# One hybrid attention and feed-forward layer: the first dilated head's preparation, the constant fills and the raw output weights are moved

## The chip, the cores and the metric

The kernel runs on one core of one Trainium2 chip. The metric is the device time of one execution in microseconds; the median of several runs is compared. The core has five engines with queues of their own: TensorE (PE, with its weight loads as PEld), VectorE (DVE), ScalarE (ACT), GpSimd (POOL) and SyncE (SP), which here issues nearly all DMA transfers.

## The reference

One encoder layer over 1024 positions of width 1024, in float32:

```
proj = rms_norm(x, norm1_g) @ w_in            -> qA(512) kA(128) vA(128) qB kB vB (512 each)
out_a = dense softmax attention: 8 q heads, 2 kv heads, QK-norm, 2-D axial rotary
out_b = 8 heads, mixture of three dilated windows (128,1) (512,4) (2048,16), ALiBi, QK-norm
x = x + concat(rms_norm(out_a), rms_norm(out_b)) @ w_out
u = conv3(rms_norm(x, norm2_g) @ w_up) + conv_b
out = x + (gelu(u[:2816]) * u[2816:]) @ w_down
```

## The kernel before, in words

All data lie in two hand-placed arenas in SBUF (`bigf` for float32, `bigr` for float32r) and one in PSUM (`ps`, eight banks); the constants O_..., F_..., R_... at the top of the file are places in them, and several tenants share a place one after another. A float32 product is made of three float32r products: each operand is split into a high part (a ScalarE copy) and a low part (a subtraction on VectorE or GpSimd).

The stages, with their time in the profile:

- *In-projection*, to about 212 us: four column chunks, seven block products each (`in_product`), with the weights prepared two products ahead (`w_prep`: a subtraction such as L382, the copy L388, the subtraction L389), results taken out of PSUM by `in_out` (ACT L420 to L428, DVE L417), and the norm and rotary of finished q and k (`done`: L490 norm, L285 turn on GpSimd, L500 and L503). Beside the last chunk the dense keys are split and transposed (`k_split` L324, `k_ready` with the transposes L177 and the ScalarE copies L332 and L333), four constants of -1 are written under the keys (`fill_k`, L348), and the first dense group is prepared.
- *Dense heads*, about 212 to 431 us: 16 groups of 13.4 us (128 queries by 4 heads). `a_prep(g + 1)` hands out the preparation of the next group in seven pieces: `nat` (L576, L577), `first` (transposes), four row maxima `mx` (products L597, maxima L598), `last` (L601, transposes, L605). `a_main(g, ...)` goes over eight key tiles: scores (L624, L625), exponential (L627), one or more pieces of the preparation according to the tuple `plan`, and the products with V of two tiles before (L619); `o_norm` (L639, L640) writes the group's output to `qab`. Group 15 prepares the first dilated head in place of a further group: 16 pieces, `b_split(0)` and the fifteen of `b_prep(0)`.
- *Dilated heads*, about 431 to 600 us: eight heads of some 20 us, eight steps each. `b_split` splits k and q of a head, `b_prep` transposes q (`trq`, copy L700) and k (`trk`, ScalarE copies L691 and L692, VectorE casts L693 and L694), takes eight row maxima (`mx`, products L707 to L712, maxima L718) and transposes the corrected low parts of q (`trl`: L726, transposes, copy L731). `b_s` makes the scores of a step: bias L747, then L759 and L761 (first four steps) or L769 and L770, the exponential L773, and for the first four steps a split (copy L775, subtraction L776). L761 and L770 read what `trl` wrote. `b_pv`, two steps behind, multiplies with V (L790, L795; out of PSUM by L798 and L802 into F_OS). The next head's `b_prep` is handed out beside the steps.
- *Output projection* to about 700 us, then up-projection, convolution, gate and down-projection. The raw rows of w_out (eight blocks, `wo_load`, L812) are loaded into places that are free for a while (`F_WOR`) and split from there into `R_WO` (`wo_split`, ScalarE L818, VectorE L819); the table `wo_early` says at which head and step.

Constants that the dilated heads need (ones and zeros around V, zeros beside the low parts of q, -1 under the keys) are the nine `fills`, of which one is handed out behind each of the first nine dense groups. `fill` multiplies any finite data by zero and adds the constant (L214, 128 rows; L926 and L348, 64 rows).

What sets the order: each engine runs a fixed list. The lists are made ahead of time by the framework's planner, which takes the program text as priority and may put an instruction earlier than its place in the text when its data and its place are free in its own reckoning. Semaphores then hold an instruction until what it depends on is done; an engine does not pass a waiting instruction.

Of the kernel before, what the change touches and what calls it, by code (L numbers as in the profile page):

```python
# [32 lines left out]
O_IDF = 0  # L33
# [62 lines left out]
F_G2 = O_F + 3584  # L96
F_HN = O_F + 4608
F_JK3 = O_F + 7840
F_WOR = [O_F + o for o in (2560, 2560, 2560, 3584, 5632, 6656, 2560, 5632)]


R_T2 = R_W
# [21 lines left out]
def tile_encoder_layer(ctx, tc, x, w_in, gains, outg, norm1_g, norm2_g, w_out, w_up, conv_w, conv_b,  # L124
# [20 lines left out]
    def f(off, n):  # L145
        return bigf[:, off:off + n]

    def r(off, n):
        return bigr[:, off:off + n]
# [11 lines left out]
    def rp(off, *dims):  # L161
        return raw_ap(bigr[:, off:off + 1], dims)
# [46 lines left out]
    def qab(tt):  # L209
        return O_QAB + 1024 * tt  # L210

    def fill(dst, n, m, c):

        vec.tensor_scalar(dst, f(O_IDF, m)[:, None, :].to_broadcast([128, n, m]), 0.0, c, op0=OP.mult, op1=OP.add)  # L214

# [127 lines left out]

    def fill_k():
        for i in range(4):
            vec.tensor_scalar(r(R_KHA + 512 * i, 512)[64:128], f(F_ROPE, 512)[64:128], 0.0, -1.0,  # L348
                              op0=OP.mult, op1=OP.add)


    def w_buf(c, half):
# [227 lines left out]
    def a_prep(g):  # L580
        b, kv = divmod(g, 2)
        q2 = R_Q2A + 512 * (g % 2)
        ql = R_QLA + 512 * (g % 2)

        def nat():
            q_nat(qab(b) + 256 * kv, 64, vec, 4, 512 * kv)

        def first():
            t = next_tr()
            for i in range(4):  # L590
                tr_r(t, i, r(R_QD + 128 * (4 * kv + i), 128))
            act(r(q2, 512), bank(t), AF.Copy)

        def mx(i):
            for hf in range(2):
                b = hf
                mm(bank(b), r(q2 + 128 * i, 128), r(R_K2A + 1024 * kv + 512 * hf, 512), start=True, stop=True)  # L597
                vec.tensor_reduce(f(SM_MC + 8 * hf + i, 1), bank(b), axis=AX.X, op=OP.max)  # L598

        def last():  # L600
            vec.tensor_tensor(rp(R_QLN + 512 * kv + 64, [128, 4]), f(SM_MC, 4), f(SM_MC + 8, 4), op=OP.max)  # L601
            t = next_tr()
            for i in range(4):
                tr_r(t, i, r(R_QLN + 128 * (4 * kv + i), 128))
            act(r(ql, 512), bank(t), AF.Copy)  # L605

        return [nat, first] + [lambda i=i: mx(i) for i in range(4)] + [last]
# [65 lines left out]
    def b_split(h):  # L673
        k3 = fp(F_KN[h % 2], [64, 8], [1, 64])
        act(rp(R_KN, [128, 8], [1, 64]), k3, AF.Copy)
        gp.tensor_tensor(rp(R_KN + 64, [128, 8], [1, 64]), k3, rfp(R_KN, [128, 8], [1, 64]), op=OP.subtract)
        q_nat(O_QAB + 512 + 64 * h, 1024, gp, 8, 0, R_QLB[h % 2])
        if h < 6:
            load_k(h + 2)
# [237 lines left out]
        eng.tensor_tensor(r(o + 512, 512), t_raw(n, i), rf(o, 512), op=OP.subtract)  # L917


    fills = []  # L920
    for c, v in ((64, 1.0), (192, 0.0)):
        for i in range(2):
            fills.append(lambda o=R_VB + 1024 * i + c, v=v: fill(rp(o, [256, 4], [1, 64]), 4, 64, v))
    fills.append(lambda: fill(rp(R_QLB[1] + 64, [128, 8], [1, 64]), 8, 64, 0.0))
    for i in range(4):
        fills.append(lambda o=R_SET[0] + 2048 + 512 * i: vec.tensor_scalar(  # L926
            r(o, 512)[64:128], f(O_QAB, 512)[64:128], 0.0, -1.0, op0=OP.mult, op1=OP.add))

    def take(prep, n):
        for _ in range(n):  # L930
# [2 lines left out]
                if p:  # L933
                    p()

    prep = [lambda: fill(rp(R_QLN + 64, [128, 8], [1, 64]), 8, 64, 0.0)] + a_prep(0)
    for i in range(4):
        kv_proj(i)
        x_rest(i)
# [94 lines left out]
    load_tabs(1)  # L1034

    tail = []
    for g in range(16):
        prep = a_prep(g + 1) if g < 15 else [lambda: b_split(0)] + b_prep(0)
        tail = a_main(g, prep, tail, late, (3, 2, 2, 2, 2, 2, 2, 1) if g == 15 else (1, 1, 1, 1, 1, 1, 1, 0),
                      (0, 1, 1, 0, 1, 0, 1, 0) if g < 3 else (0, 0, 1, 0, 1, 0, 1, 0) if g < 7 else (0, 1, 0, 0, 0, 1, 0, 0))  # L1040
        if g == 7:
            dma(f(F_CNT, 384), cnt)
            gp.memset(fp(F_VCN + 64, [66, 8]), 1.0)
            load_vc(0)
        if g == 11:
            load_k(0)
            load_k(1)
        if g == 5:
            v_split(R_VB, F_VBN)
            load_v(1)  # L1050
        take(fills, 1)
    for t in tail:
        t()
    take(prep, 99)


    wo_early = {(4, 0): [(wo_load, 0)], (4, 5): [(wo_split, 0), (wo_load, 1)], (5, 5): [(wo_split, 1), (wo_load, 2)],
                (6, 0): [(wo_load, 3)], (7, 0): [(wo_load, 4), (wo_load, 5)], (7, 1): [(wo_split, 2), (wo_load, 6)],
                (7, 3): [(wo_split, 3)], (7, 5): [(wo_split, 4), (wo_load, 7)]}

    def mixer_out_early(h, s):
        for fn, k in wo_early.get((h, s), []):
            fn(k)
        if h != 7:
            return
        if s in (0, 2):
            mix_tr(s // 2, 0)
        if s in (1, 3):
            mix_sq(s // 2, 0)
        if s == 4:  # L1070
            dma(f(F_G2, 1024), bcast(norm2_g, 1024))
        if s == 7:
            proj_out(0, 0, 0)
            proj_out(0, 0, 1)
# [381 lines left out]
```

## Time and profile before

| | |
|---|---|
| median of 3 runs | 1344.41 us (1344.02 to 1344.56) |
| the profiled execution | 1343.92 us, of it 1342.2 us span |
| TensorE busy | 1311.1 us, 98% of the span |
| VectorE, ScalarE, GpSimd busy | 991.7, 674.0, 363.4 us |
| granted TensorE clock, mean | 0.999 |

The span is the time from the first to the last recorded instruction. Times in the profile count from the span's start. TensorE is pipelined, so two of its instructions overlap in the record and "busy" is not "at its peak". A name such as L382 is a line of the kernel. In a row of a timeline stand the start, the duration (us), the engine, the line, the operation, output and inputs, and in brackets how long the engine sat idle before it and what released it.

### The profile page before, as it was taken

What the parts mean: (1) busy time and instruction counts of PE and PEld (TensorE: products, weight loads), DVE (VectorE), ACT (ScalarE), POOL (GpSimd) and SP (SyncE); (2) the same over time, 40 slices, a digit from 0 to 9 for tenths busy, and PEclk for the clock granted to TensorE, in tenths of its full rate; (3) what the DMA queues carried; (4) which work ended last, traced back from release to release, by engine and by line L of the source; (5) the groups of instructions that cost most, each with busy time, mean ns of one, the idle gap of its engine ahead of it and who ended that gap; (6) DMA issues with size and microseconds to landing.
All of it is one profiled execution on the core that took longest, in us unless ns stands there. A gap on an engine that the chain in (4) does not pass through costs nothing.

```text
span 1342.2 us, 20068 instructions
## 1 busy us (share of the span) xinstructions
PE 1311.1 (98%) x7559; PEld 1134.9 (85%) x7559; DVE 991.7 (74%) x1613; ACT 674.0 (50%) x1057; POOL 363.4 (27%) x274
## 2 busy tenths in 40 slices
PE   8999999999999999999999999999999999999998
PEld 7999989989998888878877788888888888888887
DVE  4987696864545888876579877887787789586664
ACT  7855553644445776764365444444444445244331
POOL 1611123020001222100114565556656651100000
PEclk9999999999999999999999999999999999999999
DMA  7144212000001333252222233232233325897873
GB/s 256 53 123 114 80 39 65 9 9 0 1 1 34 107 105 81 67 166 79 94 87 71 102 110 111 86 102 96 102 115 105 102 101 190 283 311 228 293 223 113
DMA packets 119859, 148.08 MB, mean 110 GB/s; under 512 B 50833, under 2 KB 76881, under 8 KB 119761
## 3 DMA queue, kind: packets, MB, share of 16 engines
q1 hardware_dynamic: 118609, 143.65, 33.3%
q0 software_dynamic: 1152, 3.15, 0.9%
q8 instruction: 59, 0.97, 0.3%
q14 instruction: 39, 0.32, 0.1%
HBM read 112.95 MB, written 33.82 MB: 109 GB/s over the span
## 4 chain that ended last, share of the span: by engine, by line
PE 70%; DVE 16%; ACT 5%; issue 4%; POOL 4%; DMA 1%; SPq 0%; DVEq 0%; ACTq 0%; POOLq 0%
PE ps L619 7%; PE ps L1161 7%; PE ps L1162 7%; PE ps L1163 7%; PE ps L1277 5%; PE ps L1276 5%; PE ps L1278 5%; DVE bigf L1194 4%; PE ps L624 2%; PE ps L597 2%; PE ps L625 2%; POOL bigf L1208 2%; PE ps L862 2%; PE ps L795 2%; PE ps L864 2%
## 5 line engine op out<-in xcount | busy, mean ns | idle before, releaser
L1161 PE MATMUL ps<-bigr 128*128 128x512 f32 x616 | 241.1, 392 | 6.6 <-DVE bigf L1165 6.1
L1162 PE MATMUL ps<-bigr 128*128 128x512 f32 x616 | 239.8, 389 | 0.0
L1163 PE MATMUL ps<-bigr 128*128 128x512 f32 x616 | 239.7, 389 | 0.0
L1144 ACT ACTIVATE bigr<-bigf 128x512 fp32r<-128x512 f32 x154 | 92.8, 624 | 159.2 <-POOL bigf L1136 95.4
L1194 DVE SCALAR_TENSOR_TENSOR bigf<-bigf 128x768 f32<-128x768 f32 (+1 forms) x176 | 146.4, 889 | 26.3 <-ACT bigf L1192 26.3
L619 PEld LDWEIGHTS ps<-bigf 128*128 128x128 f32 x1024 | 139.4, 191 | 10.5
L1161 PEld LDWEIGHTS ps<-bigr 128*128 128x128 f32 x616 | 115.6, 188 | 35.6 <-DVE bigf L1165 9.9
L1145 DVE TENSOR_TENSOR bigr<-bigf,bigr 128x512 fp32r<-128x512 f32 x112 | 116.5, 1057 | 32.6 <-ACT bigr L1144 32.6
L1256 ACT ACTIVATE bigr<-bigf 128x1024 fp32r<-128x1024 f32 x77 | 80.6, 1059 | 119.5 <-PE ps L1278 76.9
L1163 PEld LDWEIGHTS ps<-bigr 128*128 128x128 f32 x616 | 115.6, 188 | 24.2
L1162 PEld LDWEIGHTS ps<-bigr 128*128 128x128 f32 x616 | 115.6, 188 | 23.6
L619 PE MATMUL ps<-bigf 128*128 128x65 f32 x1024 | 134.3, 267 | 0.0
L405 PE MATMUL ps<-bigr 128*128 128x256 f32 x448 | 127.2, 284 | 1.2 <-ACT bigf L291 1.2
L406 PE MATMUL ps<-bigr 128*128 128x256 f32 x448 | 126.8, 283 | 0.0
L407 PE MATMUL ps<-bigr 128*128 128x256 f32 x448 | 126.7, 283 | 0.0
L627 ACT ACTIVATE bigf<-ps 128x512 f32<-128x512 f32 x128 | 75.7, 597 | 93.5 <-PE ps L625 91.1
L1277 PE MATMUL ps<-bigr 128*128 128x512 f32 x308 | 119.9, 389 | 0.0
L1278 PE MATMUL ps<-bigr 128*128 128x512 f32 x308 | 119.8, 389 | 0.0
L1276 PE MATMUL ps<-bigr 128*128 128x512 f32 x308 | 119.8, 389 | 0.0
L1257 DVE TENSOR_TENSOR bigr<-bigf,bigr 128x1024 fp32r<-128x1024 f32 x77 | 93.0, 1221 | 28.7 <-ACT bigr L1256 26.7
L598 DVE TENSOR_REDUCE bigf<-ps 128x1 f32<-128x512 f32 x128 | 86.0, 689 | 23.6 <-PE ps L597 22.2
L1208 POOL TENSOR_TENSOR bigf<-bigf 128x512 f32<-128x512 f32 x44 | 69.1, 1590 | 89.9 <-DVE bigf L1199 65.6
(221 smaller groups left out, 2892.6 us busy)
## 6 DMA issues: line engine op xcount, KB each, us to landing
bigf<-w_down SPq DMA_DIRECT2D x99, 256.0 KB, 4.3
bigf<-w_up SPq DMA_DIRECT2D x44, 512.0 KB, 4.2
bigf<-gscr SPq DMA_DIRECT2D x77, 256.0 KB, 4.1
gscr<-bigf SPq DMA_DIRECT2D x33, 512.0 KB, 2.7
bigf<-w_in SPq DMA_DIRECT2D x8, 1024.0 KB, 5.3
bigf<-x SPq DMA_DIRECT2D x15, 512.0 KB, 6.6
bigf<-tmx SPq DMA_DIRECT2D x8, 672.0 KB, 5.1
bigf<-w_out SPq DMA_DIRECT2D x8, 512.0 KB, 4.0
```

Source lines behind the costliest of these rows:

```text
L405: mm(o, ah, wh, start=(k == 0 and t % 2 == 0 and n != 2), stop=False, skip_group_check=True)
L406: mm(o, ah, wl, start=False, stop=False, skip_group_check=True)
L407: mm(o, al, wh, start=False, stop=(k == 3), skip_group_check=True)
L619: mm(bank(ob, 65, 66 * i), f(slots[kt] + 128 * i, 128), f(F_VA + 132 * kt + 66 * kv, 65), start=(kt == 0 and i == 0), stop=(kt == 7), skip ...
L1145: (gp if n in (2, 4) and m > 3 else vec).tensor_tensor(rp(o + 512, [128, 4], [1, 128]), src, rfp(o, [128, 4], [1, 128]), op=OP.subtract)
L1161: mm(bank(b), wh, th, start=(k == 0 and n in (1, 5, 6, 7)), stop=False, skip_group_check=True)
L1162: mm(bank(b), wh, tl, start=False, stop=False, skip_group_check=True)
L1163: mm(bank(b), wl, th, start=False, stop=(k == 3), skip_group_check=True)
L1194: vec.scalar_tensor_tensor(f(a + o, n), f(i + d, n), w_, f(a + o, n), op0=OP.mult, op1=OP.add)
L1276: mm(o, ah, r(d, 512), start=(q == 0 and n in (1, 5, 2)), stop=False, skip_group_check=True)
L1277: mm(o, ah, r(d + 1024, 512), start=False, stop=False, skip_group_check=True)
L1278: mm(o, al, r(d, 512), start=False, stop=(q == NQ - 1), skip_group_check=True)
```

## The change

- Of the constants, the zeros beside the dense low q (`R_QLN`) and the four of `fill_k` are written by ScalarE (Copy with scale 0 and the constant as bias) instead of VectorE.
- The nine `fills` stay on VectorE; one is handed out behind each of groups 4 to 12, and it reads the output of the group before in place of the identity or q.
- The pieces of `b_prep(0)` follow those of `a_prep(15)` in one list: four are handed out beside group 14, twelve beside group 15.
- Raw blocks 3, 4, 5 and 7 of w_out get other places (the bias tables' and the keys'); load 1 moves from head 4, step 5 to head 5, step 0, load 4 from head 7 to head 6.
- The loads of blocks 0, 1 and 2 get a one-element copy ahead of them, from the dilated heads' output F_OS into the place of the load.

```diff
-F_WOR = [O_F + o for o in (2560, 2560, 2560, 3584, 5632, 6656, 2560, 5632)]
+F_WOR = [O_F + o for o in (2560, 2560, 2560, 3616, 6304, 4960, 2560, 6304)]
...
-    def fill(dst, n, m, c):
-
-        vec.tensor_scalar(dst, f(O_IDF, m)[:, None, :].to_broadcast([128, n, m]), 0.0, c, op0=OP.mult, op1=OP.add)
+    def fill(dst, n, m, c, src=O_IDF, eng=None):
+
+        src = f(src, m)[:, None, :].to_broadcast([128, n, m])
+        if eng is None:
+            vec.tensor_scalar(dst, src, 0.0, c, op0=OP.mult, op1=OP.add)
+        else:
+            act(dst, src, AF.Copy, scale=0.0, bias=c)
...
     def fill_k():
         for i in range(4):
-            vec.tensor_scalar(r(R_KHA + 512 * i, 512)[64:128], f(F_ROPE, 512)[64:128], 0.0, -1.0,
-                              op0=OP.mult, op1=OP.add)
+            act(r(R_KHA + 512 * i, 512)[64:128], f(F_ROPE, 512)[64:128], AF.Copy, scale=0.0, bias=-1.0)
...
     fills = []
     for c, v in ((64, 1.0), (192, 0.0)):
         for i in range(2):
-            fills.append(lambda o=R_VB + 1024 * i + c, v=v: fill(rp(o, [256, 4], [1, 64]), 4, 64, v))
-    fills.append(lambda: fill(rp(R_QLB[1] + 64, [128, 8], [1, 64]), 8, 64, 0.0))
+            fills.append(lambda g, o=R_VB + 1024 * i + c, v=v: fill(rp(o, [256, 4], [1, 64]), 4, 64, v, g))
+    fills.append(lambda g: fill(rp(R_QLB[1] + 64, [128, 8], [1, 64]), 8, 64, 0.0, g))
     for i in range(4):
-        fills.append(lambda o=R_SET[0] + 2048 + 512 * i: vec.tensor_scalar(
-            r(o, 512)[64:128], f(O_QAB, 512)[64:128], 0.0, -1.0, op0=OP.mult, op1=OP.add))
+        fills.append(lambda g, o=R_SET[0] + 2048 + 512 * i: vec.tensor_scalar(
+            r(o, 512)[64:128], f(g, 64)[64:128][:, None, :].to_broadcast([64, 8, 64]), 0.0, -1.0,
+            op0=OP.mult, op1=OP.add))
...
-    prep = [lambda: fill(rp(R_QLN + 64, [128, 8], [1, 64]), 8, 64, 0.0)] + a_prep(0)
+    prep = [lambda: fill(rp(R_QLN + 64, [128, 8], [1, 64]), 8, 64, 0.0, eng=act)] + a_prep(0)
...
     tail = []
+    prep = []
     for g in range(16):
-        prep = a_prep(g + 1) if g < 15 else [lambda: b_split(0)] + b_prep(0)
-        tail = a_main(g, prep, tail, late, (3, 2, 2, 2, 2, 2, 2, 1) if g == 15 else (1, 1, 1, 1, 1, 1, 1, 0),
+
+        prep += a_prep(g + 1) if g < 15 else []
+        if g == 14:
+            prep += [lambda: b_split(0)] + b_prep(0)
+        tail = a_main(g, prep, tail, late, {14: (1, 1, 1, 1, 1, 2, 2, 2), 15: (2, 2, 2, 2, 1, 1, 1, 1)}.get(
+            g, (1, 1, 1, 1, 1, 1, 1, 0)),
...
-        take(fills, 1)
+        if g > 3 and fills:
+            fills.pop(0)(qab((g - 1) // 2) + 256 * ((g - 1) % 2))
...
-    wo_early = {(4, 0): [(wo_load, 0)], (4, 5): [(wo_split, 0), (wo_load, 1)], (5, 5): [(wo_split, 1), (wo_load, 2)],
-                (6, 0): [(wo_load, 3)], (7, 0): [(wo_load, 4), (wo_load, 5)], (7, 1): [(wo_split, 2), (wo_load, 6)],
+    wo_early = {(4, 0): [(wo_load, 0)], (4, 5): [(wo_split, 0)], (5, 0): [(wo_load, 1)], (5, 5): [(wo_split, 1), (wo_load, 2)],
+                (6, 0): [(wo_load, 3), (wo_load, 4)], (7, 0): [(wo_load, 5)], (7, 1): [(wo_split, 2), (wo_load, 6)],
                 (7, 3): [(wo_split, 3)], (7, 5): [(wo_split, 4), (wo_load, 7)]}
 
     def mixer_out_early(h, s):
         for fn, k in wo_early.get((h, s), []):
+            if fn is wo_load and h < 6:
+
+                vec.tensor_copy(f(F_WOR[k], 1), f(F_OS, 1))
             fn(k)
```

## Prediction

> **What bounds the kernel now.** The page first, to see which engine sets the time, and then the busy time by stretches, to see where that engine is not fed (columns: stretch, its length, then busy us and number of instructions of PE, PEld, DVE, ACT, POOL, then the granted TensorE clock, the DMA share and GB/s).
>
> ```profile
> PE 1311.1 (98%) x7559; PEld 1134.9 (85%) x7559; DVE 991.7 (74%) x1613; ACT 674.0 (50%) x1057; POOL 363.4 (27%) x274
> 376.50:390.00 13.50, 13.50 (x99) 12.40 (x99) 6.60 (x12) 6.35 (x12) 0.00 (x0) 1.00 0.00 0
> 180.00:184.00 4.00, 4.00 (x36) 4.00 (x36) 3.88 (x7) 0.00 (x0) 4.00 (x7) 1.00 0.01 2
> 188.00:192.00 4.00, 2.62 (x23) 2.62 (x24) 4.00 (x5) 4.00 (x7) 0.00 (x0) 1.00 0.01 4
> 196.00:200.00 4.00, 3.10 (x25) 2.80 (x23) 3.96 (x5) 2.65 (x6) 1.27 (x1) 1.00 0.48 135
> 436.00:438.00 2.00, 0.81 (x4) 0.61 (x4) 1.97 (x3) 2.00 (x5) 0.00 (x0) 0.84 0.53 220
> 438.00:440.00 2.00, 2.00 (x9) 1.74 (x9) 1.88 (x3) 1.98 (x4) 0.43 (x1) 0.50 0.47 115
> 440.00:442.00 2.00, 2.00 (x16) 2.00 (x16) 1.87 (x6) 1.51 (x3) 0.87 (x1) 0.81 0.38 151
> ```
>
> TensorE is busy in 98% of the span, so the change adds or removes no time by making other engines do less; it can only fill the 31 us (1342.2 - 1311.1) in which TensorE is idle, or spare it the slow clock. In a dense group (second row) it is never idle and VectorE and ScalarE are half free. The two places that the change touches are holes: the end of the in-projection (180 to 200 us), where VectorE is full, and the hand-over from the dense to the dilated heads (432 to 442), where the clock falls to 0.50 as well.
>
> The timeline of TensorE gives the size of each hole and who ended it (the bracket: idle time before, and its releaser).
>
> ```profile
> 189.38 0.53 PE L177 MATMUL ps<-bigr 128*128 128x128 f32 x4 [1.67 <-ACT bigr L333]
> 198.64 0.70 PE L597 MATMUL ps<-bigr 128*128 128x512 f32 x2 [0.90 <-DVE bigf L417]
> 200.41 0.50 PE L597 MATMUL ps<-bigr 128*128 128x512 f32 x1 [0.24 <-DVE bigf L598]
> 431.98 0.28 PE L712 MATMUL ps<-bigr 128*128 128x256 f32 x1
> 433.34 0.84 PE L177 MATMUL ps<-bigr 128*128 128x128 f32 x8 [0.35 <-ACT bigr L700]
> 435.02 0.39 PE L761 MATMUL ps<-bigr 128*128 128x256 f32 x1 [0.84 <-ACT bigr L731]
> 437.55 0.73 PE L711 MATMUL ps<-bigr 128*128 128x432 f32 x1 [1.19 <-ACT bigr L691]
> PE ps L707 <- DVE bigf L718: 0.6, 1, 0.6
> ```
>
> First hole: 1.67 + 0.90 + 0.24 = 2.81 us. Second: 0.35 + 0.84 + 1.19 + 0.6 (from the view of waits between 430 and 448 us) = 3.0 us, and by the three clock rows (0.16 + 0.50 + 0.19) x 2 us = 1.7 us of clock: 4.7 us.
>
> One more fact decides how the text is to be read: the planner does not keep its order. Five of the constants of L214 stand behind dense groups 0 to 4 in the text and ran by 196 us (L214 x5 in the next fence but one), before the first group; the first loads of w_out stand in head 4 and were issued at the hand-over (the first two, and their splits):
>
> ```profile
> 431.57 0.35 SPq L812 DMA_DIRECT2D bigf<-w_out  x1
> 437.99 0.33 SPq L812 DMA_DIRECT2D bigf<-w_out  x1
> 435.33 1.16 ACT L818 ACTIVATE bigr<-bigf 128x1024 fp32r<-128x1024 f32 x1
> 443.63 1.14 ACT L818 ACTIVATE bigr<-bigf 128x1024 fp32r<-128x1024 f32 x1
> L775 ACT ACTIVATE bigr<-ps 128x512 fp32r<-128x512 f32 x32 | 19.1, 605 | 0.3
> L776 DVE TENSOR_TENSOR bigr<-ps,bigr 128x512 fp32r<-128x512 f32 x32 | 21.8, 681 | 11.9 <-ACT bigr L775 11.2
> ```
>
> What has no wait of its own goes as soon as its place is free; so a false read ("bound to") is what moves such work.
>
> **The change, part by part.**
>
> *Constants.* The chain of waits between 178 and 200 us lies wholly on VectorE; these are its pieces that the change takes away, and what follows them:
>
> ```profile
> 179.91 0.34 DVE bigr L214
> 180.63 0.65 DVE bigr L348
> 181.65 0.64 DVE bigr L348
> 183.71 1.19 DVE bigr L348 x2
> 184.91 1.39 DVE bigf L382
> 186.31 1.13 DVE bigf L500
> 194.99 1.14 DVE bigr L214 x5
> 186.40 1.07 ACT L388 ACTIVATE bigr<-bigf 128x1024 fp32r<-128x1024 f32 x1 [7.84 <-DVE bigf L382]
> 188.74 0.58 ACT L333 ACTIVATE bigr<-ps 64x512 fp32r<-64x512 f32 x1
> 179.97 5.25 POOL L285 TENSOR_TENSOR bigf<-bigf 128x128 f32<-128x128 f32 x8 [11.25 <-DVE bigf L192]
> 234.15 1.31 POOL L676 TENSOR_TENSOR bigr<-bigf,bigr 128x512 fp32r<-128x512 f32 x1 [5.65 <-ACT bigr L675]
> L576 ACT ACTIVATE bigr<-bigf 128x512 fp32r<-128x512 f32 x16 | 10.1, 632 | 4.8 <-DVE bigf L192 4.8
> L926 DVE TENSOR_SCALAR bigr<-bigf x4: 424/424/425, 244.8 to 251.8; 64x512 fp32r<-64x512 f32 x4
> ```
>
> Ahead of L382 go 0.34 + 0.65 + 0.64 + 1.19 = 2.82 us, and 1.14 us later. ScalarE had waited 7.84 us for L382 with the copies of L424, L332 and L333 queued behind it, and L333 is what TensorE waited 1.67 us for: with L382 2.8 us earlier that wait is gone. What is late next is VectorE again: L500 behind L382 reads what GpSimd turns until 185.2 us (179.97 + 5.25), so VectorE behind it gains about 1 us of the 2.8 (L500 starts at 186.3), plus the 1.14: some 2.1 us against the 0.90 wait, which came from that queue. I take -2.2 us. Ends: 0 (the order turns out so that L333 stays late) and -2.8 (all of the hole).
>
> The five constants on ScalarE cost 5 x 0.63 = 3.2 us (the row of L576, the same size) and lie in its 7.84 us wait: nothing. If the planner puts them behind L388 instead, up to 2.5 us (5 starts some 0.5 apart) come back on the queue of L333; that is inside the upper end. The five other constants of L214 and the four of L926 (0.42 each) go to groups 4 to 12, one in each, on a VectorE that is busy 6.60 of 13.50 us there; they read what VectorE itself wrote one group earlier, so nobody waits: nothing. Without that cover it would be 9 x 0.42 = 3.8 us.
>
> The Trainium skill's page "ScalarE: Activation LUTs", section "Rules for kernel authors", speaks against this step: simple adds and multiplies belong on VectorE. By it alone the five constants would lose 5 x (0.63 - 0.42) = 1 us of engine time, and the sum would be 1 us worse; the trace agrees with the price of one and not with the loss, since ScalarE stands idle there.
>
> *Head 0 prepared beside two groups.* No instruction is added. Before, all 16 pieces stand in group 15; now 4 (the split, one set of q transposes, both sets of k) stand in group 14 and 12 in group 15, the last row maxima in its last quarter but one. In the profile the eighth maximum's product is at 431.98 (L712), as the dense stage ends, and then TensorE has nothing that does not need its result: VectorE's maximum, the transposes, ScalarE's L731, and only then L761. This string of 0.35 + 0.84 falls away if the maxima are done by some 428. The first k split ran at 234 us already (L676, above), its reload on SP behind it, and neither moves; the reload of tmx behind the last maximum only comes earlier on SP. Group 14 gets 4 casts and 5 copies more; both engines are half free.
>
> *Loads of w_out bound to heads 4 and 5.* The splits at 435.33 and 443.63 take 1.16 + 1.14 us out of ScalarE's queue at the hand-over, where it is full (2.00 of 2.00 at 436), directly ahead of the exponentials and of L691, which TensorE waited 1.19 for; their VectorE halves go too. What stays is the filling of the new stage: an exponential of about the length of the copy behind it, that copy (0.6, L775 above) and the subtraction (0.7, L776) before the first product with V, partly beside the last dense products. Of 4.7 us I let 1.2 stay (one copy and one subtraction): -3.5. Ends -1.5 (stalls as now except the splits' 1.19 and a part) and -4.7.
>
> The splits come back in heads 4 and 5, where a stretch reads (first row; below it a split at the end of head 7, the landing of w_out, and a wait of ScalarE for a load elsewhere)
>
> ```profile
> 520.00:540.00 20.00, 19.39 (x139) 16.58 (x137) 17.07 (x53) 13.20 (x25) 4.45 (x4) 1.00 0.34 90
> 587.10 0.50 PE L790 MATMUL ps<-bigr 128*128 128x256 f32 x2 [0.86 <-ACT bigr L775]
> 585.44 1.13 ACT L818 ACTIVATE bigr<-bigf 128x1024 fp32r<-128x1024 f32 x1
> DMA to landing us min/median/max: 3.5/4.0/4.5
> ACT bigf L364 <- DMA bigf<-w_in: 10.3, 5, 3.4
> ```
>
> ScalarE has 6 us free in 20, VectorE 3. A split that stood badly at 585.44 cost TensorE 0.86. For two of them I take +0.4, ends 0 and 2 x 1.13 = +2.3. The three one-element copies on VectorE are instructions of under 0.2 us that read a finished F_OS: nothing; ScalarE's next write of F_OS waits for them, VectorE's own queue is behind them. On SP the loads stand among a head's seven small loads, with about 15 us to spare.
>
> *New places.* Load 4 can go when head 6 begins instead of after the maxima of head 7, so its split leaves the crowded end; 5 to 7 still wait for the last matmuls on the places they overwrite. -0.2, ends 0 and -0.9 (the 0.86).
>
> Sum: -2.2 - 3.5 + 0.4 - 0.2 = -5.5 us on the profiled execution's 1343.92 (its span 1342.2 and 1.7 around it): 1338.4; the median of the runs is 0.5 above that execution: **1338.9**.
>
> **The rivals.**
>
> (1) *The hand-over stays starved and the clock falls again.* A head's start needs one q and four k copies and two casts on ScalarE and VectorE beside the first exponentials; with no products of an earlier head to cover them, TensorE may be starved all the same, only without the splits. For it: ScalarE at 2.00 of 2.00. Against: heads in the middle have the same copies and run at 1.00 (520 to 540 us). Then the 1.7 of clock and about half of the 3.0 stay: -1.5 there, -2.2 - 1.5 + 0.4 = -3.3 or, if the first hole closes only in part, -2.5: about 1341.5.
>
> The Trainium skill's "TensorE: Matmul & The Clock Gate", section "Part 1: The HAM clock gate", says that one window of about 3.4 us without enough work halves the clock until a full busy one; by it the 1.7 us stay whole or go whole. The trace agrees so far: 2.62 of 4.00 busy at 188 kept 1.00, 0.81 of 2.00 at 436 did not.
>
> (2) *The first hole stays*, because it was only partly VectorE's queue (GpSimd until 185.2): -3.3, 1341.1. Against: the 7.84 us wait names L382.
>
> (3) *ScalarE waits for a load, slower.* The planner sets a split behind a load that is now due just then; ScalarE's queue is in order, and the exponentials stand behind it. That it can happen shows L364 (10.3 us in 5 waits). Price: three bound loads, up to 4.0 us of landing each, of which 0.86 of 1.13 reach TensorE: 9.1 us, net +3.6: 1348. It decides from about 7 us of such waits (5.5 / 0.76). Against: five of a head's eight steps, some 12 of its 20 us, lie between load and split, and the view of waits has no split that waited for a load before.
>
> (4) *Nothing moves*: the bound reads are done early and the planner puts everything back: 1344. What reads a group's output can't be early, so this has little weight.
>
> **Chances.** Forecast 0.57; rival 1 0.17 (0.10 of it within the bound); rival 2 0.10 (0.02); rival 3 0.12; rival 4 0.04. With 0.2% (2.7 us) as about what a measurement of this kernel can tell from no change: faster 0.72, same 0.16, slower 0.12. Range: down to all good ends (-2.8 - 4.7 - 0.9 = -8.4, 1336.0), up through rivals 1 and 2 with what they leave open, 1343.2.
>
> **What would show it.** Right: ScalarE's wait before L388 shorter by over 2 us, no wait on L333; five constants of ScalarE before 184 us; the last L718 of head 0 before the last L619; no L818 before 500 us; clock 1.00 throughout 430 to 450. Wrong: a PE wait on L773 or L775 of over 1 us at the hand-over, clock under 0.9 there, an ACT wait on w_out in heads 4 to 6, or new idle TensorE time after 600 us, where nothing is changed.

## The result, and the profile after

| | before | changed |
|---|---|---|
| median (20 runs each) | 1344.33 us (1343.40 to 1346.29) | 1346.73 us (1344.54 to 1348.27) |
| ratio | | 1.0016, 95% interval 1.0011 to 1.0022 |
| the profiled execution | 1343.92, span 1342.2 | 1344.82, span 1343.1 |

The kernel did not gain 5.5 us; it lost 2.4 by the medians. In the changed kernel a line stands two to five places further down: L333 is L337, L388 L391, L417 L420, L285 L289, L500 L503, L598 L601, L597 L600, L619 L622, L639 L642, L691 L694, L718 L721, L747 L750, L776 L779, L818 and L819 L821 and L822, L1018 L1023.

First the page's busy times and the stretches of the prediction again, in the changed kernel (columns as there).

```profile
PE 1310.2 (98%) x7559; PEld 1133.0 (84%) x7559; DVE 987.9 (74%) x1611; ACT 676.8 (50%) x1062; POOL 361.8 (27%) x274
```

```profile
180.00:184.00 4.00, 4.00 (x37) 4.00 (x36) 1.57 (x4) 1.69 (x2) 3.85 (x7) 1.00 0.01 2
188.00:192.00 4.00, 4.00 (x36) 4.00 (x35) 4.00 (x7) 2.74 (x5) 0.00 (x0) 1.00 0.02 4
196.00:200.00 4.00, 2.04 (x12) 1.73 (x13) 3.97 (x5) 1.66 (x4) 2.24 (x1) 1.00 0.64 208
436.00:438.00 2.00, 1.62 (x6) 1.06 (x7) 1.52 (x4) 2.00 (x6) 0.00 (x0) 1.00 0.00 0
438.00:440.00 2.00, 1.98 (x18) 1.83 (x16) 2.00 (x5) 1.93 (x4) 0.94 (x1) 1.00 0.02 4
440.00:442.00 2.00, 1.62 (x14) 1.48 (x12) 1.72 (x6) 2.00 (x5) 0.67 (x2) 1.00 0.24 56
520.00:540.00 20.00, 18.80 (x136) 16.17 (x134) 17.21 (x54) 13.53 (x25) 4.46 (x4) 1.00 0.34 94
```

TensorE's total is as before. Both holes look as wanted: TensorE is busy 4.00 of 4.00 at 188 (2.62 before), and the clock is 1.00 at 436 to 442 (0.50 before). But 196 to 200 has only 2.04 us of work (3.10 before), and a head in the middle 18.80 of 20 (19.39).

The timeline of TensorE in the changed kernel names the new waits.

```profile
197.72 0.70 PE L600 MATMUL ps<-bigr 128*128 128x512 f32 x2 [2.27 <-ACT bigr L670]
440.55 0.50 PE L750 MATMUL ps<-bigr 128*128 128x256 f32 x2 [0.38 <-DVE bigr L779]
526.14 0.33 PE L710 MATMUL ps<-bigr 128*128 128x144 f32 x1 [0.77 <-DVE bigf L721]
547.17 0.34 PE L710 MATMUL ps<-bigr 128*128 128x144 f32 x1 [0.77 <-DVE bigf L721]
569.28 0.40 PE L710 MATMUL ps<-bigr 128*128 128x288 f32 x1 [0.62 <-DVE bigf L721]
588.54 0.50 PE L750 MATMUL ps<-bigr 128*128 128x512 f32 x1 [0.94 <-DVE bigr L779]
```

The view puts the wait of 2.27 us down to ScalarE's L670. It is read here as a wait for VectorE: in all sixteen profiles that have a wait at this product, VectorE's second L420 (L417 before) ended 0.14 or 0.15 us ahead of it. The last row stands where TensorE waited 0.86 us (587.10) and then 0.22 before.

The signs that the prediction named are there as well; ScalarE's and VectorE's timelines:

```profile
180.02 0.63 ACT L352 ACTIVATE bigr<-bigf 64x512 fp32r<-64x512 f32 x1
181.32 1.06 ACT L391 ACTIVATE bigr<-bigf 128x1024 fp32r<-128x1024 f32 x1 [0.67 <-DVE bigf L385]
523.05 1.19 ACT L821 ACTIVATE bigr<-bigf 128x1024 fp32r<-128x1024 f32 x1
431.61 0.42 DVE L721 CUSTOM_DVE_ANT_0 bigf<-ps,bigf 128x256 bf16<-128x256 f32 x1
```

The last of ScalarE's constants (L352) is over before 184 us, its wait for VectorE there is 0.67 (7.84 before), the first split of w_out (L821) comes at 523, and head 0's last row maximum (L721) ends at 432.0, before the last dense products do. All of these look at the places where a gain was expected; the loss is elsewhere.

To see what each stage gave, the trace is cut where TensorE begins the first score product of a group or a head, and last where it begins the last product with V. Of each kernel, before and then changed, four stretches: groups 0 to 13, groups 14 and 15, heads 0 to 3, heads 4 to 7.

```profile
211.63:401.02 189.39, 187.38 (x1331) 170.91 (x1329) 113.89 (x191) 93.78 (x161) 21.89 (x23) 1.00 0.04 10
401.02:431.86 30.84, 30.84 (x235) 28.86 (x235) 16.26 (x47) 16.38 (x29) 3.86 (x3) 1.00 0.04 10
431.86:513.71 81.85, 78.12 (x547) 68.11 (x546) 69.07 (x209) 57.21 (x102) 17.76 (x16) 0.98 0.37 101
513.71:597.90 84.19, 82.02 (x563) 69.56 (x562) 67.74 (x183) 57.94 (x102) 10.17 (x9) 1.00 0.36 101
```

```profile
210.74:402.05 191.31, 188.28 (x1330) 170.85 (x1329) 114.67 (x196) 93.76 (x161) 21.09 (x23) 1.00 0.04 10
402.05:432.99 30.94, 30.94 (x236) 28.96 (x236) 17.15 (x52) 16.38 (x29) 3.85 (x3) 1.00 0.04 10
432.99:512.78 79.79, 77.38 (x547) 66.79 (x545) 65.24 (x199) 55.01 (x100) 17.73 (x16) 1.00 0.33 85
512.78:599.53 86.75, 81.97 (x563) 69.65 (x562) 71.47 (x192) 59.87 (x104) 10.19 (x9) 1.00 0.39 111
```

TensorE does the same products in each pair, give or take one that a trace lacks; the lengths differ by +1.9, +0.1, -2.1, +2.6. With the in-projection's end (41.78 to 41.31 us: -0.5), the start of the output projection (8.68 to 8.05: -0.6), and the start-up, which ended 0.4 earlier in this execution, that is the 0.9 us by which the profiled span grew.

The median grew by 2.4. In the profiled execution the clock was 1.00 throughout; the runs with a mean clock of 1.000 (7 of 20) averaged 1345.1 us, the 13 with 0.999 or 0.998 averaged 1347.2. Where the clock falls is shown below, and why the mean alone does not settle it.

### The profile page after: what moved, and what is told of

It reads as the page before. It is cut to its first block, busy times and chain, and to the rows that moved or that the text cites. A ratio compares the mean times of both kernels' runs of the same rounds, so it can differ in the third digit from the quotient of the medians.

```text
span 1343.1 us, 20072 instructions
## 1 busy us (share of the span) xinstructions
PE 1310.2 (98%) x7559; PEld 1133.0 (84%) x7559; DVE 987.9 (74%) x1611; ACT 676.8 (50%) x1062; POOL 361.8 (27%) x274
## 4 chain that ended last, share of the span: by engine, by line
PE 78%; DVE 11%; ACT 5%; issue 3%; POOL 2%; DMA 1%; SPq 0%; ACTq 0%; DVEq 0%; POOLq 0%
PE ps L1175 10%; PE ps L1176 10%; PE ps L1177 9%; PE ps L622 7%; PE ps L1292 5%; PE ps L1290 5%; PE ps L1291 5%; PE ps L627 2%; PE ps L600 2%; PE ps L628 2%; PE ps L798 2%; PE ps L865 2%; PE ps L867 2%; PE ps L866 2%; PE ps L408 1%
## 5 line engine op out<-in xcount | busy, mean ns | idle before, releaser
L622 PEld LDWEIGHTS ps<-bigf 128*128 128x128 f32 x1024 | 138.8, 191 | 10.3
L622 PE MATMUL ps<-bigf 128*128 128x65 f32 x1024 | 134.1, 267 | 0.0
L601 DVE TENSOR_REDUCE bigf<-ps 128x1 f32<-128x512 f32 x128 | 86.1, 689 | 20.6 <-PE ps L600 19.0
```

The costliest lines, as they stand in the source:

```text
L622: mm(bank(ob, 65, 66 * i), f(slots[kt] + 128 * i, 128), f(F_VA + 132 * kt + 66 * kv, 65), start=(kt == 0 and i == 0), stop=(kt == 7), skip ...
```

## The experiments

Two theories stood against each other: (A) each stage's loss belongs to the part of the change that touches it; (B) any edit reshuffles the planned lists by 1 to 2 us. The kernel before ran beside each set of four (medians 1343.61, 1344.42, 1343.81, 1344.26). The table gives for each run the length of the stages cut as above (us), from its profile, with the stretches in which its clock stood at 0.50.

| run | median | ratio (95%) | end of in-projection | groups 0-13 | groups 14-15 | heads 0-3 | heads 4-7 | half clock from |
|---|---|---|---|---|---|---|---|---|
| before | | | 41.78 | 189.38 | 30.85 | 81.85 | 84.19 | 437.4 |
| changed | 1346.73 | 1.0016 | 41.31 | 191.31 | 30.94 | 79.79 | 86.76 | none |
| e4 (changed, again) | 1347.39 | 1.0031 (1.0020 to 1.0041) | 41.99 | 191.26 | 30.94 | 79.75 | 86.78 | 198.8 |
| e1 constants | 1346.34 | 1.0018 (1.0008 to 1.0027) | 40.60 | 194.48 | 30.85 | 81.73 | 84.20 | 275.2 (double), 442.4 |
| e9 ScalarE constants | 1345.01 | 1.0016 (1.0007 to 1.0025) | 42.91 | 189.33 | 30.86 | 81.12 | 84.22 | 200.2 |
| e8 bound fills | 1346.66 | 1.0017 (1.0008 to 1.0026) | 42.11 | 192.87 | 30.84 | 82.17 | 84.20 | 191.1, 276.4, 443.6 |
| e2 head 0's preparation | 1346.81 | 1.0022 (1.0013 to 1.0031) | 41.67 | 189.35 | 30.96 | 80.21 | 88.47 | 579.5 |
| e3 raw output weights | 1345.62 | 1.0014 (1.0006 to 1.0023) | 41.73 | 189.33 | 30.85 | 80.81 | 86.74 | none |
| e5 both, no constants | 1344.43 | 1.0000 (0.9992 to 1.0009) | 42.09 | 189.37 | 30.95 | 79.75 | 86.76 | 190.0 |
| e10 no bound fills | 1345.05 | 1.0011 (1.0002 to 1.0020) | 43.97 | 189.37 | 30.93 | 79.78 | 86.74 | 198.9 (double) |
| e6 changed, GpSimd | 1348.56 | 1.0038 (1.0025 to 1.0050) | 40.88 | 191.32 | 30.93 | 79.77 | 90.84 | none |
| e7 e5, GpSimd | 1349.41 | 1.0037 (1.0025 to 1.0050) | 41.91 | 189.32 | 30.94 | 79.73 | 92.42 | 530.5 |
| e11 e5, halves | 1343.08 | 0.9997 (0.9988 to 1.0005) | 41.73 | 189.33 | 30.92 | 79.77 | 85.63 | none |
| e16 e11 again | 1342.92 | 0.9991 (0.9982 to 0.9999) | 41.77 | 189.36 | 30.95 | 79.77 | 85.64 | none |
| e12 e10, halves | 1343.77 | 1.0004 (0.9995 to 1.0012) | 44.31 | 189.32 | 30.94 | 79.73 | 85.64 | 199.7 (double) |
| e13 e9, turn | 1342.85 | 0.9991 (0.9983 to 1.0000) | 40.48 | 189.41 | 30.85 | 81.16 | 84.20 | none |
| e14 e12, turn | 1342.05 | 0.9987 (0.9978 to 0.9996) | 40.55 | 189.43 | 30.95 | 79.77 | 85.60 | none |
| e15 e11, turn | 1343.37 | 0.9994 (0.9985 to 1.0003) | 42.44 | 189.37 | 30.96 | 79.75 | 85.63 | none |

"Double" is a stretch of 6.8 us, every other one is 3.4 us. Half clock at the very end of the span, at most its last 2.0 us (e3), is left out of the last column; it alone makes the mean clock 0.999 in the profiles of e3 and e13. The columns already settle much: from group 0 on a stage has the same length to 0.1 us in every kernel with the same parts (189.3 without bound fills, 79.8 with both other parts, 86.7 with the raw weights), apart from the half-clock stretches. That speaks for A; heads 4 to 7 of e2 are the exception. The end of the in-projection is less even: 40.60 to 41.31 us in e1, e6 and the changed kernel, which have the same constants and no half clock there.

**The three parts by themselves, and all again (e1 to e4).** e1 holds the edits of `fill`, `fill_k` and `fills`; e2 only those of `prep` and the plans; e3 only `F_WOR`, `wo_early` and the one-element copies.

> Only the constants are changed (five on ScalarE, nine bound to groups 4 to 12). Theory A (each stage's loss belongs to the part of the change that touches it): the in-projection is 0.5 us shorter (the 1.67 us wait goes, a new wait for the product behind ScalarE's table load takes 1.4 back), dense groups 3 to 5 are 1.9 us longer as in the changed kernel, the hand-over keeps its stalls and its half-clock window: about 1345.7. Theory B (any edit reshuffles the planner's lists by 1 to 2 us here and there): groups 3 to 5 are not longer in the same place, and the dilated heads differ from before by over 1 us although nothing in them is edited.

> Only head 0's preparation is spread over groups 14 and 15. Theory A: the stalls of 0.35 and 0.84 at the hand-over go, the two splits stay in ScalarE's queue there, the clock does not fall: 1.2 to 2.9 us less, about 1342.3; heads 2 to 7 as before. Theory B: the hand-over gains the same, but heads 2 to 7 lose 1 us or more without any edit there: 1344 or more.

> Only the raw output weights are changed (places, bound loads). Theory A: the hand-over loses the splits' 1.2 us of stall, heads 4 and 5 gain 0.8 us of TensorE idle each right behind the split's VectorE half, the clock window at the hand-over stays: about 1344.5. Theory B: the loss in the heads lies elsewhere than behind the splits.

> The changed kernel once more, for its clock. If a half-clock window explains why most of its executions are 2 us longer than the profiled one, this profile (if it is of such an execution) has a window at 0.50 for 3.4 us, at a place where TensorE is starved: at the hand-over, or where the waits of 0.8 us and more stand (526, 547, 569, 588 us). 1346.7 again as the median.

Each part alone is slower than the kernel before: e1 by 2.7 us, e2 by 3.2, e3 by 2.0. A had e1 slower by some 1.4, e2 faster and e3 about level, so all three are misses in size and e2 in direction. In e4 a stretch of half clock was found, but at 198.8, a place that the expectation had not named. e2 looked like B, since its loss lies in heads 4 to 7, which it does not touch. The timelines of ScalarE and TensorE there, and the stretch behind, in e2:

```profile
577.42 1.15 ACT L818 ACTIVATE bigr<-bigf 128x1024 fp32r<-128x1024 f32 x1 [2.20 <-DMA bigf<-w_out]
579.62 0.79 PE L862 MATMUL ps<-bigr 128*128 128x512 f32 x1 [2.25 <-ACT bigr L203]
```

```profile
580.00:582.00 2.00, 2.00 (x7) 1.53 (x7) 1.88 (x4) 1.13 (x3) 0.00 (x0) 0.50 0.87 221
```

A split stands in ScalarE's queue behind a load that has not landed (2.20 us), L203 stands behind the split, TensorE waits 2.25 us for it, and the clock falls to 0.50 for 3.4 us. This is rival 3 of the prediction, in the kernel without the edit of the raw weights. With that edit beside it no split waits for a load (e5, the changed kernel), so the two parts belong together: e2 and e3 lose 4.3 and 2.6 us in those heads, e5 with both 2.6. Which piece of that edit keeps the wait away, and why e2's lists changed so far from its own lines, was not tried.

**Without the constants, and the splits on GpSimd (e5 to e7), bound fills alone (e8).** e6 and e7 replace the VectorE half of the first four splits:

```diff
-        vec.scalar_tensor_tensor(r(R_WO[k] + 1024, 1024), raw, g, rf(R_WO[k], 1024), op0=OP.mult, op1=OP.subtract)
+        if k < 4:
+            gp.tensor_scalar(raw, raw, g, None, op0=OP.mult)
+            gp.tensor_tensor(r(R_WO[k] + 1024, 1024), raw, rf(R_WO[k], 1024), op=OP.subtract)
+        else:
+            vec.scalar_tensor_tensor(...)
```

> The change without its constants: only the preparation of head 0 beside two groups and the raw output weights. Theory A (each stage's loss belongs to the part that touches it): the end of the in-projection and groups 3 to 5 read as in the kernel before (waits of 1.67 and 0.90, no wait of 2 us before the first maxima products, no idle time over 1.3 us before group 4), the hand-over keeps its gain of about 2 us up to head 4, and heads 4 to 7 lose about 2.5 us to waits of 0.6 to 0.8 before the maxima products; the sum is 0 to -1 against the kernel before, so 1342.6 to 1343.6 with 1343.6 for the kernel before. Theory B (any edit reshuffles the planned lists by 1 to 2 us): 1345 or more, with idle time in a stage that no part of this edit touches.

> The changed kernel, with the VectorE half of the first four splits of w_out (1.27 us each on VectorE) given to GpSimd as a multiplication in place and a subtraction. Theory A: the three waits of 0.77, 0.77 and 0.62 before the maxima products of heads 5 to 7 go, and heads 4 to 7 shorten by about 2 us: 2 us less than the changed kernel, about 1345. Theory B: the lists change elsewhere and at least as much is lost in another place: 1347 as the changed kernel. GpSimd is under a quarter busy there; if its longer instructions make the split late for the output projection, there is a wait before the first projection products instead.

> Both edits: no constants moved, and the VectorE half of the first four splits on GpSimd. Theory A: the gain of the hand-over stands alone, -2 to -3.5 against the kernel before, 1340 to 1341.6 with 1343.6 before. Theory B: 1344 or more.

> One half of the constants alone: the nine fills of VectorE bound to groups 4 to 12, the five others still on VectorE in the in-projection. Theory A with the ScalarE constants as the cause of the wait of 2.27 us before the first maxima products: the wait of 1.67 before the key transposes stays, that wait is not there and the groups run as before: 1343 to 1344. Theory A with the bound fills as the cause: idle time of about 1.3 to 1.7 us in groups 3 to 5 appears here as well, 1345. Theory B: idle time in stages without fills.

e5 stands level with the kernel before, at the upper end of what A had expected: -2.1 in heads 0 to 3, +2.6 in heads 4 to 7. e8 has the +1.9 of groups 0 to 13 (the rest of its 3.5 is the half-clock stretch) and, in the in-projection, the old wait before the key transposes: moving the nine fills causes the former, as A's second branch said. By single groups, group 3 is 1.0 us longer, group 4 1.3 longer and group 5 0.35 shorter; the other groups are as before. The view of TensorE's waits between 251 and 295 us (us in total, times, longest), first before, then the changed kernel:

```profile
PE ps L597 <- DVE bigf L598: 1.1, 1, 1.1
```

```profile
PE ps L600 <- DVE bigf L601: 2.0, 3, 1.3
```

TensorE waits longer for row maxima. It is not the bound fills themselves that hold these up: the first of them runs at 279.00, at the end of group 4, when most of the loss is over (timelines of VectorE before, of VectorE and of TensorE in the changed kernel).

```profile
254.88 1.40 DVE L598 TENSOR_REDUCE bigf<-ps 128x1 f32<-128x512 f32 x2 [0.54 <-PE ps L597]
258.12 1.29 DVE L598 TENSOR_REDUCE bigf<-ps 128x1 f32<-128x512 f32 x2 [1.30 <-PE ps L597]
```

```profile
254.18 0.18 DVE L642 RECIPROCAL bigf<-ps 128x4 f32<-128x4 f32 x1 [1.99 <-PE ps L622]
254.46 1.29 DVE L601 TENSOR_REDUCE bigf<-ps 128x1 f32<-128x512 f32 x2
256.00 1.97 DVE L601 TENSOR_REDUCE bigf<-ps 128x1 f32<-128x512 f32 x3
279.00 0.28 DVE L216 TENSOR_SCALAR bigr<-bigf 128x256 fp32r<-128x256 f32 x1
```

```profile
255.21 1.09 PE L600 MATMUL ps<-bigr 128*128 128x512 f32 x2 [0.25 <-DVE bigf L601]
256.73 0.50 PE L600 MATMUL ps<-bigr 128*128 128x512 f32 x1 [0.43 <-DVE bigf L601]
```

In group 3, VectorE takes two maxima and is idle for 1.30 us before the next two in the kernel before; in the changed one TensorE's list has five maxima products between 253.95 and 256.73, and VectorE, at some 0.6 us each, does not keep up. The reciprocal L642 of `o_norm`, which now stands ahead of these maxima and waits 1.99 us, does not explain it: the first maximum starts 0.51 us after its product starts in both kernels (254.37 and 254.88, 253.95 and 254.46). Nor did a bound fill draw it forward: this `o_norm` writes group 2's output, and the first bound fill reads group 3's. What differs ahead of group 3 is what was taken away. VectorE's instructions come in the same order in the kernel before and in e8, but for five fills that are missing at 195 us, until 244.8 us, where the first of four more (L926) is missing; from there the order is another one. That the edit of the fills causes the loss is shown by e8, e9 and e10; why the planner's new list is the worse one was not tried.

e6 and e7 went the other way than A expected: the waits before the maxima products shrank, and heads 4 to 7 got longer by 4 to 6 us. Timelines of VectorE and GpSimd in e6:

```profile
526.68 2.20 DVE L729 TENSOR_TENSOR bigr<-bigf 128x4 fp32r<-128x4 f32 x1
526.50 2.36 POOL L824 TENSOR_TENSOR bigr<-bigf,bigr 128x1024 fp32r<-128x1024 f32 x1
```

```profile
PE ps L177 <- DVE bigr L729: 4.5, 3, 1.6
```

A VectorE instruction on 4 columns (the larger of two inputs), 0.15 us in the changed kernel, takes 2.20 us and ends when GpSimd's long subtraction ends; TensorE waits for it (the second fence, from the view of waits between 513 and 600 us: 4.5 us in three times). So this pair of runs refuted the remedy and left the diagnosis open.

**The other half of the constants (e9), all without bound fills (e10), and the diagnosis with another remedy (e11, e12).** The remedy is two short instructions in place of the long one, so that a row maximum can go between:

```diff
-        vec.scalar_tensor_tensor(r(R_WO[k] + 1024, 1024), raw, g, rf(R_WO[k], 1024), op0=OP.mult, op1=OP.subtract)
+        for c in range(0, 1024, 512):
+            vec.scalar_tensor_tensor(r(R_WO[k] + 1024 + c, 512), f(F_WOR[k] + c, 512), g, rf(R_WO[k] + c, 512), op0=OP.mult,
+                                     op1=OP.subtract)
```

> The other half of the constants alone: five on ScalarE, the nine fills of VectorE as before. Theory A: the wait of 1.67 us before the key transposes goes, a wait of about 2 us before the first maxima products comes in its place, groups 3 to 5 read as in the kernel before; net 0 to -1 us in the profile, so -0.5 against the kernel before, or +1 to +1.5 if the new wait draws a window of half clock. Theory B: idle time in groups 3 to 5 or in the dilated heads.

> The changed kernel without the bound fills (the nine stand as in the kernel before). Theory A: groups 3 to 5 read as in the kernel before, 1.4 us less than the changed kernel, heads 4 to 7 keep their waits: -0.5 against the kernel before, +0.5 if the in-projection draws a window of half clock. Theory B: 1346 or more with 1344.4 before.

> No constants moved; head 0 prepared beside two groups, raw output weights as changed, and the VectorE half of each split of w_out as two instructions of 128x512 in place of one of 128x1024. Theory A: the waits of 0.77, 0.77 and 0.62 before the maxima products of heads 5 to 7 fall to under 0.2 each, so about 2 us less than the same kernel with whole halves, which stood level with the kernel before: -2 (1342.4 with 1344.4 before). Theory B: 1344 or more, with the idle time in another place.

> The changed kernel without the bound fills and with the VectorE half of each split in two. Theory A: as the kernel without constants and with halves, -2, and 0 to -1 more for the ScalarE constants, or +1 where their new wait draws a window of half clock: 1341.4 to 1343.4 with 1344.4 before. Theory B: 1344 or more.

In the changed kernel, VectorE and then the same TensorE wait with the long and (e11) with the short pieces:

```profile
524.27 1.28 DVE L822 SCALAR_TENSOR_TENSOR bigr<-bigf,bigr 128x1024 fp32r<-128x1024 f32 x1 [0.27 <-ACT bigr L821]
525.48 0.60 DVE L721 CUSTOM_DVE_ANT_1 bigf<-ps,bigf 128x432 bf16<-128x432 f32 x1
```

```profile
524.51 0.34 PE L707 MATMUL ps<-bigr 128*128 128x144 f32 x1 [0.34 <-DVE bigf L718]
545.35 0.34 PE L707 MATMUL ps<-bigr 128*128 128x144 f32 x1 [0.29 <-DVE bigf L718]
```

The waits fell from 0.77, 0.77 and 0.62 to 0.34, 0.29 and under 0.15, while the one at the end of head 7 grew from 0.94 to 1.12; heads 4 to 7 fell by 1.1 us, not by the 2 expected; the median stood 0.7 below that of the kernel before (1.3 in e16), where e5 stood level. The diagnosis holds, for less than half of the 2.6 us; the rest stays open. e9 came out as A had it (+1.2), e10 and e12 0.7 and 1.0 above A's upper ends. Their profiles show half clock for twice as long in the in-projection; but these two executions (1347.34 and 1346.12) were among the longest of their kernels, so that this also holds for the medians is argued. All three confirm the split of the constants: groups as before, and the wait at the first maxima product comes with the ScalarE constants, 2.49 us with half clock behind it (timeline of TensorE and a stretch in e9):

```profile
199.81 0.85 PE L600 MATMUL ps<-bigr 128*128 128x512 f32 x2 [2.49 <-DVE bigf L420]
```

```profile
200.00:202.00 2.00, 2.00 (x9) 1.72 (x8) 2.00 (x2) 0.00 (x0) 0.78 (x1) 0.55 0.96 349
```

**Why taking work off VectorE did not shorten its queue (e13 to e15), and e11 again (e16).** The queues of VectorE, GpSimd and ScalarE, at first two rows of the kernel before and VectorE's in e8, then the changed kernel:

```profile
195.05 1.05 ACT L388 ACTIVATE bigr<-bigf 128x1024 fp32r<-128x1024 f32 x1
196.13 1.23 DVE L389 TENSOR_TENSOR bigr<-bigf,bigr 128x1024 fp32r<-128x1024 f32 x1
```

```profile
196.64 1.23 DVE L393 TENSOR_TENSOR bigr<-bigf,bigr 128x1024 fp32r<-128x1024 f32 x1 [1.14 <-ACT bigr L392]
```

```profile
184.51 1.23 DVE L503 TENSOR_TENSOR bigf<-bigf 128x1024 f32<-128x1024 f32 x1 [2.94 <-POOL bigf L289]
195.22 1.23 DVE L392 TENSOR_TENSOR bigr<-bigf,bigr 128x1024 fp32r<-128x1024 f32 x1 [0.71 <-ACT bigr L391]
196.36 1.22 DVE L420 TENSOR_TENSOR bigf<-ps,bigf 128x1024 f32<-128x1024 f32 x1
180.15 4.33 POOL L289 TENSOR_TENSOR bigf<-bigf 128x128 f32<-128x128 f32 x8 [11.25 <-DVE bigf L192]
192.74 1.28 ACT L1023 ACT_TABLE_LOAD   x1
194.14 1.04 ACT L391 ACTIVATE bigr<-bigf 128x1024 fp32r<-128x1024 f32 x1
```

VectorE lost 2.82 + 1.14 = 4.0 us of constants and gained 2.94 + 0.71 = 3.65 us of waiting: for GpSimd's rotary turn, and for a split behind ScalarE's table load. The L420 that the first maxima product waits for starts at 196.36, where before it started at 197.28; half of these 0.9 us is the earlier start-up. TensorE, 2.3 us ahead of the kernel before by then, ran dry at 195.45 and waited until 197.72. Measured from the start of GpSimd's turn, so that the start-up drops out, this L420 (L417) starts after 17.3 us in the kernel before and in all others in which these constants and the turn are the old ones, e8 too; after 16.6 with ScalarE's constants (e9, e10, e12), after 16.2 with all constants moved (changed, e1, e4, e6). The edit gives four of the eight operations of that turn to VectorE, which stands idle beside them:

```diff
-            rot(so + ss * i, o + 1024 * i, 4, tab + ts * i)
+            rot(so + ss * i, o + 1024 * i, 4, tab + ts * i, vec if (c, t0, u) == (2, 0, 1) and i > 1 else gp)
```

> Five constants on ScalarE alone, and of the second set of rotary turns four of eight operations on VectorE in place of GpSimd. If GpSimd's turn is the bound behind the constants: VectorE's wait of 2.94 us for it falls under 1 us, the chain behind it starts 1.5 to 2 us earlier, and the wait before the first maxima products falls from 2.5 to under 1 us: in-projection 1 to 2 us shorter than with the five constants alone, -1 to -2 against the kernel before. If the order of the lists is the cause: a wait of about 2 us stays there, +1 as with the five constants alone.

> The changed kernel without bound fills, with the splits' VectorE halves in two and half of that turn on VectorE. Turn as the bound: -2 to -3 against the kernel before. Order of the lists: 0, as without the edit of the turn.

> No constants moved, head 0 beside two groups, raw weights, splits in halves, half of that turn on VectorE. VectorE is then more loaded ahead of the key transposes: the wait of 1.67 us there stays or grows by up to 1 us; -0.7 to +0.5 against the kernel before by both theories.

> The kernel without moved constants and with the splits in halves once more: -0.7 to -1.2 against the kernel before, as its profile had it.

TensorE, VectorE and GpSimd in e13:

```profile
181.12 1.96 DVE L289 TENSOR_TENSOR bigf<-bigf 128x128 f32<-128x128 f32 x4
180.13 2.81 POOL L289 TENSOR_TENSOR bigf<-bigf 128x128 f32<-128x128 f32 x4 [11.26 <-DVE bigf L192]
197.24 0.70 PE L600 MATMUL ps<-bigr 128*128 128x512 f32 x2 [1.45 <-ACT bigr L670]
```

VectorE no longer waits for GpSimd, the later wait is 1.45 in place of 2.49, the half clock behind it is gone, and the in-projection is 1.3 us shorter than before (2.4 shorter than e9). From the start of the turn, L420 starts after 15.7 us in e13 (15.8 in e14), 0.8 earlier than with ScalarE's constants alone. The turn was a bound on that queue; the wait of 1.45, not under 1 as expected, stays, and how much of the gain in the medians is the missing half clock is not separated. Beside the old constants (e15) the same edit gains nothing, as expected: 17.8 us. e14, all that pays of the change with the two mends, is at 0.9987 (0.9978 to 0.9996): 2.2 us below the kernel before by the medians, as expected of it, and the lowest ratio, though its interval overlaps those of e13 and e16; it leaves out the bound fills. e15 and e16 came out near their expectations too (-0.9 and -1.3).

## Why the prediction was wrong, step by step

It said 1338.9 us (1336.0 to 1343.2); 1346.73 lies above the range and above rivals 1 and 2, on the side of the slower ones, but not by the mechanism of rival 3.

- **The in-projection's hole, -2.2: measured -0.5.** Right was that the wait on L333 goes (1.67 to none) and ScalarE takes the five constants in its own idle time. The step that failed is "VectorE behind it gains about 1 us of the 2.8 (L500 starts at 186.3), plus the 1.14: some 2.1 us against the 0.90 wait". From the start of the turn, VectorE gained 0.7 (17.3 to 16.6) and, with the 1.14 as well, 1.1 (16.2). The 1.14 alone gained nothing (e8): the subtraction behind these constants reads a split that ScalarE ended at 196.10, and it started at 196.13; without the five, in e8, it waits the same 1.14 us for that split. I had seen that GpSimd's turn would end the gain, but counted the two holes as two. They are one queue: freed of the 1.67, TensorE comes to the first maxima product earlier and waits there for the same VectorE result. How far ahead it comes differs between executions: with the same queue (16.2) the stage was 0.5 us shorter than before in the changed kernel, 0.9 in e6, 1.2 in e1, and 0.2 longer in e4, with half clock.
- **Constants of groups 4 to 12, "nothing": measured +1.9 (189.38 to 191.31; e8 has it and e9 does not).** That "nobody waits" for the fills held; no wait in the profile is put down to one. The step that failed looked only at the place the constants go to, and put at nothing what taking them from their old places does: from the first missing one on the lists have another order, in which TensorE's maxima products stand closer than VectorE can follow. Some 1.0 us more idle time of TensorE is recorded in groups 3 and 4. Why the planner orders it so stays open.
- **The hand-over, -3.5: measured -2.0** (groups 14 to head 3). The mechanism was right: clock 1.00, the splits of w_out gone to 523 us and later, no wait on what L761 reads, and 0.12 us on the copy L691 in place of 1.19. Two sizes were off. The clock: e9 and e13 keep all the waits of the hand-over and only lose the half-clock stretch, and heads 0 to 3 are 81.1 us in them against 81.85, so it cost 0.7 and not 1.7. Half clock covers time in which TensorE waits anyway. The waits: 81.1 to 79.8, thus 1.3 and not 1.8; a part came back in pieces such as the 0.38 before L750, on a ScalarE that is still at 2.00 of 2.00. The condition "if the maxima are done by some 428" was not met, since the last starts at 431.6, 0.9 earlier than before; the waits of 0.35 and 0.84 went all the same. The dense products there end after that maximum (432.9 against 432.0); before, they ended ahead of it (431.5 against 432.9).
- **The splits in heads 4 and 5, +0.4 (end +2.3): measured +2.6.** The step that failed priced them on ScalarE. It is the VectorE half, 1.28 us in one piece ahead of a row maximum, that TensorE waited for; VectorE was free 3 us in 20, but not at that moment. e11 shows it as far as its 1.1 us go; the other 1.5 stays open.
- **New places, -0.2: no gain can be read.** The wait at the end of head 7 by which this was priced did not go: 0.86 and 0.22 before, 0.94 in the changed kernel and in e3. From the last product with V to the second block of the output projection it took 8.05 to 8.66 us in the profiles with the new places, and 7.92 to 8.68 in those without.
- **The range.** Its upper end, 1343.2, has no sum behind it. The bad ends that the prediction itself named (0, -1.5, +2.3 and 0) add up to +0.8, which is 1345.2; the measured median lies 1.5 above that as well.
- **Rivals.** 1 (the clock falls again at the hand-over) and 2 (the first hole stays) did not happen as told, though the first hole came back 8 us later. 3 happened in e2 only. None named another order of the lists in groups 3 and 4, and none the half clock that a *new* hole brings, in the in-projection or the groups. The profiles show it there in e4 (198.8), e9, e10 and e12, and within the changed kernel's runs 1345.1 us go with a mean clock of 1.000 and 1347.2 with less. That this is the whole distance from the profile's +0.9 to the median's +2.4 is argued, since most runs have no trace and half clock at the end of the span lowers the mean too; in e5 the runs with a mean clock of 1.000 and those with 0.998 average the same 1344.3 us. Why the same kernel falls into it in some executions stays open.

## What to carry to other kernels

Work taken off a full queue is worth only the distance to the next releaser of that queue: look up what the first instruction behind it waits for, and when that is ready, before counting the work as gain, and treat two waits on one queue as one. Work that leaves its place in a planned list lets others come forward there; look at the old place as well as at the new one. And price a moved instruction on every engine it uses by its longest piece, not by the idle share of the stretch that takes it up.

## What the runs showed of the hardware

- The clock was halved for 3.41 us at a time, or twice that, apart from the end of the span. At the end of the in-projection it followed waits of TensorE of 1.87 (e5), 1.93 (e10), 1.94 (e8), 1.96 (e4), 2.17 (e12) and 2.49 us (e9), but not the 2.27 us of the changed kernel's own profile, and none of the eleven profiles in which the longest wait there was 1.84 us or less. The Trainium skill's "TensorE: Matmul & The Clock Gate", section "Part 1: The HAM clock gate", says that the clock is halved after an idle window of about 3.4 us and full again after a busy one. The trace agrees with the length; the waits ahead of the stretches here were shorter, 1.87 to 2.49 us.
- What such a stretch costs depends on its place: 1.6 us where TensorE was fed (groups 0 to 13: 192.87 in e8, 191.31 in the changed kernel), 0.6 to 1.0 where it waited anyway (heads 0 to 3: 81.73, 81.85 and 82.17 in e1, before and e8, against 81.12 in e9).
- A short VectorE instruction can take 15 times its time beside a long one on GpSimd (2.20 us against 0.15, above), and ends with it. The Trainium skill's "SBUF — State Buffer", section "SBUF: two separate sides", states that a VectorE instruction with two SBUF inputs and a GpSimd one that reads SBUF lock each other out for a whole instruction; the trace agrees, with a start 0.18 us behind GpSimd's and an end 0.02 behind.
